# Spreading copies moved between row blocks, and one PSUM tile per bank for odd heads, in a softmax-times-V kernel

## The chip, the cores and the metric

One NeuronCore of a Trainium2 chip runs the kernel. The metric is device time in microseconds (us), as the median of several executions; times inside an execution come from its profile, counted from the start of the profiled span (about 2 us shorter than the device time). The engines are called PE (matmuls), PEld (the weight loads of PE), DVE (VectorE), ACT (ScalarE), POOL (GpSimd) and SP (which issues all DMAs here). The granted clock is the share of its full clock that PE was given, as the profile records it.

## The reference

```python
# scores: (8, 12, 1024, 1024) fp32, v: (8, 12, 1024, 64) fp32; 96 heads in all
attn = np.exp(scores - np.max(scores, axis=-1, keepdims=True))
attn = attn / (np.sum(attn, axis=-1, keepdims=True) + 1e-8)
return np.matmul(attn, v).astype(np.float32)
```

The kernel leaves out the maximum (the scores are normal draws) and gets the row sums from a column of ones beside v.

## The kernel before

The loop takes four heads per pass, 24 passes in all. A head has eight row blocks of 128 rows. For each block ACT makes exponentials in fp16 (`p_nat`, two blocks per instruction), PE transposes them in eight pieces into PSUM (`psT`), DVE copies them to SBUF (`pt`, "pt copy" below), and two blocks later PE multiplies them with v (`psO`). At the end of a head DVE normalises: one reciprocal and two multiplications into `out_sb`. The fourth head of a pass is normalised in two halves, after its fourth and its eighth block.

v arrives by one DMA per pass, on other partitions than the products need. Four small DVE copies per head ("spreading copies") move it there.

```python
psT_bufs = buffers(ps_pool, 4, [P, SK], FP16, "psT")            # 4 banks
psO_bufs = buffers(ps_pool, 2, [P, R // G, 512], FP32, "psO")   # 2 x 2 banks; R // G = 2
...
def normalise(k, st, first, last):
    psO = st["psO"][:, first:last, 0 : G * M].rearrange("p b (g m) -> p b g m", m=M)
    recip = st["recip"][:, first:last]
    nc.vector.reciprocal(out=recip, in_=psO[:, :, :, D : D + 1])
    ...                                     # T = 2 multiplications into out_sb
def finish(u):                              # products of one row block
    ...
    for c in range(C):
        nc.tensor.matmul(out=st["psO"][:, b, g * M : (g + 1) * M],
                         lhsT=pt[:, c * P : (c + 1) * P], rhs=st["vones"][:, c, 0:M], ...)
    if k == AHEAD - 1:                      # fourth head: bank by bank
        if g == G - 1:
            normalise(k, st, b, b + 1)
    elif r == R - 1:
        normalise(k, st, 0, R // G)
...
def spread_v(k):
    for s in range(S):                      # S = 4
        nc.vector.tensor_copy(
            out=vones_bufs[k][s * Q : (s + 1) * Q, :, 0:D].rearrange("i (h l) d -> i h l d", l=L),
            in_=v_half[k * Q : (k + 1) * Q, :, s])
def last(n0):                               # loads and store at the end of a pass
    ...                                     # last pass but one:
            load(AHEAD - 2, BH - 2, (4, 4))
            load(AHEAD - 1, BH - 1, (2, 2, 2, 1, 1))    # the last head's scores in five pieces
            store(n0, AHEAD - T)
def heads(n0):
    for k in range(AHEAD):                  # AHEAD = 4
        spread_v(k)
        st = dict(vones=vones_bufs[k])
        for r in range(R):                  # R = 8
            ...                             # exponentials, transposes into psT
            nc.vector.tensor_copy(out=pt[:], in_=psT[:])
            ...                             # finish() of the block two before
    ...
    cast_v()                                # POOL: v of the next pass to fp16
    last(n0)
```

Written once per head, the spreading copies depend on nothing that the pass makes, and the framework's scheduler puts all sixteen of a pass at its start.

The softmax here doesn't subtract the row's maximum and nothing guards it: scores larger than these inputs give would overflow.

## Time and profile before

| | before |
|---|---|
| device time, median | 1070.0 us (1069.4 to 1070.8) |
| DMA queue, share of 16 engines' span | 98.8% |
| DVE / ACT / PE / PEld busy | 73% / 69% / 67% / 62% |
| a spreading copy | 285 ns, 16 in a pass |
| a pt copy | 688 ns, 32 in a pass |
| last exponential ends | 1052.35 us |
| last multiplication ends | 1063.34 us |
| span | 1067.8 us |

The first two rows say that the run is a stream of bytes. The last three say that the work after the stream takes some 15 us, and only there can other engines show. The prediction shows the lines and reads them.

### The profile page before, as it was taken

The numbers are of one execution on the slowest core, as the hardware profiler recorded it, in microseconds if no ns is written. First come the engines' busy times: TensorE is split into PE (matmuls) and PEld (weight loads), VectorE is DVE, ScalarE is ACT, GpSimd is POOL, SyncE is SP. The second block draws the span as 40 slices with busy tenths as digits, with TensorE's granted clock in tenths as the row PEclk, the third lists the DMA queues.
The fourth block names the chain that finished last, engine by engine and source line by source line (L and its number), as shares of the span: only waits on it lengthen the run. The fifth ranks groups of instructions, "written<-read, shape, count | busy, mean of one in ns | idle before, by whom it ended". The sixth has DMA issues, their size and how long they took to land.

```text
span 1067.8 us, 32453 instructions
## 1 busy us (share of the span) xinstructions
PE 713.4 (67%) x12288; PEld 663.8 (62%) x12288; DVE 775.3 (73%) x1517; ACT 735.8 (69%) x432; POOL 48.1 (5%) x31
## 2 busy tenths in 40 slices
PE   3765757667676567665766757667676677675765
PEld 2755756656666567665766756656666566665665
DVE  3675867777677677777776867767777777777677
ACT  3756776666867667586666776666867667586684
POOL 0000000000000000000000000000000000000000
PEclk9888868898698897987878869888788787977889
DMA  9999999999999999999999999999999999999994
GB/s 393 431 425 434 422 442 432 432 432 429 435 431 432 432 432 425 439 432 432 432 431 434 424 440 432 432 432 430 434 432 432 432 432 426 438 432 432 432 425 173
DMA packets 24915, 453.05 MB, mean 424 GB/s; under 512 B 2768, under 2 KB 2768, under 8 KB 9168
## 3 DMA queue, kind: packets, MB, share of 16 engines
q1 hardware_dynamic: 24912, 453.00, 98.8%
q8 instruction: 3, 0.05, 0.0%
HBM read 436.21 MB, written 25.17 MB: 432 GB/s over the span
## 4 chain that ended last, share of the span: by engine, by line
DMA 78%; ACT 12%; PEld 4%; PE 2%; DVE 2%; issue 1%; SPq 0%; ACTq 0%; DVEq 0%; PEldq 0%
DMA s_nat<-in_scores_dram 78%; ACT p_nat L243 12%; PEld L255 3%; PEld L136 1%; PE psT L255 1%; DVE pt L261 1%; PE psO L136 1%; DVE vones L200 0%; SPq L176 0%; DVE out_sb L121 0%; ACTq L243 0%; SPq L188 0%; DVE recip L116 0%; DVEq L224 0%; PEldq L217 0%
## 5 line engine op out<-in xcount | busy, mean ns | idle before, releaser
L243 ACT ACTIVATE p_nat<-s_nat 128x2048 f16<-128x2048 f32 (+1 forms) x408 | 705.0, 1800 | 226.5 <-DMA s_nat<-in_scores_dram 200.6
L261 DVE COPY pt<-psT 128x1024 f16<-128x1024 f16 x768 | 511.3, 688 | 221.8 <-PE psO L136 96.7
L255 PE MATMUL psT<-order,p_nat 128*128 128x128 f16 x6144 | 550.2, 245 | 165.0 <-ACT p_nat L243 161.6
L255 PEld LDWEIGHTS <-p_nat 128*128 128x128 f16 x6144 | 441.2, 123 | 177.4 <-ACT p_nat L243 177.0
L136 PE MATMUL psO<-vones,pt 128*128 128x65 f16 x6144 | 356.7, 204 | 183.0 <-DVE pt L261 132.9
L136 PEld LDWEIGHTS <-pt 128*128 128x128 f16 x6144 | 291.5, 106 | 220.0 <-DVE pt L261 171.3
L121 DVE TENSOR_TENSOR out_sb<-psO,recip 64x512 f32<-64x512 f32 (+1 forms) x240 | 139.7, 582 | 7.8
L200 DVE COPY vones<-v_half 32x512 f16<-32x512 f16 x384 | 109.4, 285 | 23.2 <-POOL v_half L195 6.0
L243 ACT ACT_TABLE_LOAD x24 | 30.8, 1283 | 90.1 <-DMA s_nat<-in_scores_dram 82.0
L195 POOL CAST v_half<-v_sb 128x2048 f16<-128x2048 f32 x25 | 47.4, 1897 | 994.4 <-DMA v_sb<-in_v_dram 574.6
L116 DVE RECIPROCAL recip<-psO 128x8 f32<-128x8 f32 (+1 forms) x120 | 22.7, 189 | 34.0 <-PE psO L136 34.0
L71 DVE MEMSET vones<- 128x16 f16 x4 | 0.2, 72 | 0.8 <-PEq L295 0.8
L62 DVE CAST order<-ident 128x128 f16<-128x128 f32 x1 | 0.2, 227 | 0.4 <-POOL ident masks.py:199 0.4
masks.py:199 POOL TENSOR_SCALAR_AFFINE_SELECT ident<-ident 128x128 f32<-128x128 f32 x1 | 0.3, 294 | 0.1
masks.py:197 POOL MEMSET ident<- 128x128 f32 x1 | 0.2, 205 | 0.3 <-POOLq L295 0.3
L295 POOL MEMSET const-float32-0.0<- 128x1 f32 x1 | 0.1, 99 | 0.2 <-issue 0.2
L295 POOL MEMSET const-bfloat16-1.0<- 128x1 bf16 x1 | 0.1, 103 | 0.0
L295 POOL MEMSET const-uint8-127<- 128x1 uint8 x1 | 0.1, 103 | 0.0
L295 POOL MEMSET const-float32-1.0<- 128x1 f32 x1 | 0.1, 99 | 0.0
## 6 DMA issues: line engine op xcount, KB each, us to landing
s_nat<-in_scores_dram SPq DMA_DIRECT2D x96, 4096.0 KB, 36.0
v_sb<-in_v_dram SPq DMA_DIRECT2D x24, 1024.0 KB, 37.6
out_dram<-out_sb SPq DMA_DIRECT2D x48, 512.0 KB, 27.8
s_nat<-in_scores_dram SPq DMA_DIRECT2D x2, 2048.0 KB, 33.6
s_nat<-in_scores_dram SPq DMA_DIRECT2D x3, 1024.0 KB, 32.7
s_nat<-in_scores_dram SPq DMA_DIRECT2D x2, 512.0 KB
```

The source lines that it names most:

```text
L62: nc.vector.tensor_copy(out=order16[:].rearrange("p (t j) -> p t j", t=T), in_=ident32[:].rearrange("p (j t) -> p t j", t=T),)
L71: nc.vector.memset(vo[:, :, D : D + 2], 1.0)
L116: nc.vector.reciprocal(out=recip, in_=psO[:, :, :, D : D + 1])
L121: nc.vector.tensor_tensor(out=rows.rearrange("j (b g) d -> j b g d", g=G), in0=psO[part, :, :, 0:D], in1=recip[part].to_broadcast([W, last ...
L136: nc.tensor.matmul(out=st["psO"][:, b, g * M : (g + 1) * M], lhsT=pt[:, c * P : (c + 1) * P], rhs=st["vones"][:, c, 0:M], start=(c == 0), ...
L195: nc.gpsimd.tensor_copy(out=v_half[:], in_=v_sb[:])
L200: nc.vector.tensor_copy(out=vones_bufs[k][s * Q : (s + 1) * Q, :, 0:D].rearrange("i (h l) d -> i h l d", l=L), in_=v_half[k * Q : (k + 1) ...
L243: nc.scalar.activation(out=p_nat[:, g : g + rows, :].rearrange("p r (x v) -> p x r v", v=Q * L), in_=s_bufs[k][:, r + g : r + g + rows, :] ...
L255: nc.tensor.transpose(out=psT[:, c * P : (c + 1) * P], in_=p_row[:, c // L, c % L, :], identity=order16[:],)
L261: nc.vector.tensor_copy(out=pt[:], in_=psT[:])
L295: nc = _bacc.Bacc("TRN2", target_bir_lowering=False, num_devices=1)
```

## The change

Two things are intended: DVE should not hold up the first row blocks of a pass for 5 us of spreading copies, and PE should not wait for the normalising of one bank before it writes the other.

```diff
-    psO_bufs = buffers(ps_pool, 2, [P, R // G, 512], FP32, "psO")
+    psO_whole = ps_pool.tile([P, R // G, 512], FP32, name="psO_whole")
+    psO_banks = buffers(ps_pool, R // G, [P, 1, 512], FP32, "psO")
...
 def normalise(k, st, first, last):
-        psO = st["psO"][:, first:last, 0 : G * M].rearrange("p b (g m) -> p b g m", m=M)
+        psO = psO_whole if k % 2 == 0 else psO_banks[first]
+        psO = psO[:, :, 0 : G * M].rearrange("p b (g m) -> p b g m", m=M)
...
-        if k == AHEAD - 1:
+        if k % 2 == 1:
             if g == G - 1:
                 normalise(k, st, b, b + 1)
...
 def heads(n0):
         for k in range(AHEAD):
-            spread_v(k)
+            if k == 0:
+                for s in range(S):
+                    spread_v(k, s)
...
-                nc.vector.tensor_copy(out=pt[:], in_=psT[:])
+                copy = nc.vector.tensor_copy(out=pt[:], in_=psT[:])
+                if k < AHEAD - 1 and r % (R // S) == 0:
+                    spread_v(k + 1, r // (R // S), copy)
```

`spread_v(k, s, behind)` now makes one copy and, with `behind`, gives the scheduler an order edge (no semaphore): not before that pt copy. The PSUM use stays at eight banks. Not in the intent, but in the diff: the second head of a pass is now normalised in halves too.

## The prediction

> **What bounds the kernel now.** I read the page's slices and queue part first, because a kernel with four engines near 70% may be bound by none of them.
>
> ```profile
> DMA  9999999999999999999999999999999999999994
> GB/s 393 431 425 434 422 442 432 432 432 429 435 431 432 432 432 425 439 432 432 432 431 434 424 440 432 432 432 430 434 432 432 432 432 426 438 432 432 432 425 173
> q1 hardware_dynamic: 24912, 453.00, 98.8%
> ```
>
> The DMA engines are full in every slice but the last, at a flat 432 GB/s. The chain of work in order of time says the same for one pass of the loop (four heads):
>
> ```profile
> 922.24 1.92 ACT p_nat L243
> 925.88 3.78 ACT p_nat L243 x3
> 929.79 36.02 DMA s_nat<-in_scores_dram
> 965.92 1.92 ACT p_nat L243
> ```
>
> One pass is 965.92 - 922.24 = 43.68 us, of which a load of scores is 36 us. It moves 16.8 MB of scores, 1.05 MB of v and 1.05 MB of results: 18.9 MB / 432 GB/s = 43.7 us. So 24 x 43.68 = 1048 us are bytes, and nothing on VectorE can shorten them. What is left is the start (the first load is on its way at 2 us) and what follows the last byte. Next I cut the tail into windows (columns: stretch, length, busy time of PE, PEld, DVE, ACT, POOL, granted clock, DMA share, GB/s):
>
> ```profile
> 1046.00:1048.00 2.00, 2.00 (x45) 2.00 (x42) 1.93 (x4) 2.00 (x2) 0.00 (x0) 1.00 1.01 416
> 1048.00:1050.00 2.00, 1.08 (x23) 0.77 (x22) 1.97 (x4) 1.96 (x2) 0.00 (x0) 1.00 0.71 291
> 1054.00:1062.00 8.00, 4.89 (x106) 4.44 (x103) 6.64 (x13) 0.00 (x0) 0.00 (x0) 1.00 0.05 19
> 1064.00:1066.00 2.00, 0.00 (x0) 0.00 (x0) 0.00 (x0) 0.00 (x0) 0.00 (x0) 0.59 0.64 262
> ```
>
> The scores are in by about 1051, yet the span ends at 1067.8. DVE is the busiest engine in between (6.64 of 8 us). The timeline of the last pass (heads 92 to 95) shows why it is late:
>
> ```profile
> 1024.70 5.03 DVE L200 COPY vones<-v_half 32x512 f16<-32x512 f16 x16 [0.58 <-PE L255]
> 1029.76 1.89 DVE L261 COPY pt<-psT 128x1024 f16<-128x1024 f16 x3
> 1030.20 22.15 ACT L243 ACTIVATE p_nat<-s_nat 128x2048 f16<-128x2048 f32 x13 [1.09 <-DMA s_nat<-in_scores_dram]
> 1037.16 0.69 DVE L261 COPY pt<-psT 128x1024 f16<-128x1024 f16 x1 [0.27 <-PE L136]
> 1038.12 0.69 DVE L261 COPY pt<-psT 128x1024 f16<-128x1024 f16 x1 [0.27 <-PE L136]
> 1038.72 0.20 DVE L116 RECIPROCAL recip<-psO 128x8 f32<-128x8 f32 x1
> 1039.08 0.69 DVE L261 COPY pt<-psT 128x1024 f16<-128x1024 f16 x1 [0.15 <-PE L136]
> 1048.29 3.21 DVE L261 COPY pt<-psT 128x1024 f16<-128x1024 f16 x5
> 1060.16 1.18 PE L136 MATMUL psO<-vones,pt 128*128 128x65 f16 x32 [1.64 <-DVE out_sb L121]
> 1062.25 0.18 DVE L116 RECIPROCAL recip<-psO 128x4 f32<-128x4 f32 x1 [1.42 <-PE psO L136]
> ```
>
> Four things are to be seen. All sixteen spreading copies of the four heads run in one piece at the pass's start, not four per head, and hold the first pt copy until 1029.76. The exponentials of heads 93 to 95 run without a break and end at 1052.35, 8 us before the last pt copy (1060.14), so VectorE trails. A pt copy alone has 0.27 us idle before it (pitch 0.96), while in a run of several the pitch is 3.21/5 = 0.64; the reciprocal at 1038.72 fell into such a gap and the next copy still began 0.27 after the end of the one before (1038.12 + 0.69 + 0.27 = 1039.08), so small work fits in there. And the last head's products of row blocks 4 to 7 all wait, 32 of them, until bank 0 is normalised. This last wait is in every pass:
>
> ```profile
> PE psO L136 <- DVE out_sb L121: 43.7, 24, 2.0
> ```
>
> **What the Trainium skill says.** "DMA: Bandwidth & Descriptors", Specifications, has a fabric ceiling of 435 GB/s; the trace's 432 agrees, and is above the limit of about 358 GB/s for HBM per core in the same table, so here (one core running) the measurement decides. "PSUM — Partial Sum Buffer", PSUM bank collisions raise a hardware error, asks to guard by bank and quadrant and says that different banks run clean: so products into bank 1 need not wait for reads of bank 0, and the wait above comes of the tile spanning both. "VectorE: DVE Perf Modes", Side-by-side: where the cycles go, gives about 158 cycles at 0.96 GHz on top of the elements; as an estimate from that page, a spreading copy (512 fp16 at 4 per cycle) is (128 + 158)/0.96 = 298 ns and a pt copy out of PSUM (1024 at 2 per cycle) 698 ns; the groups have 285 and 688. It agrees, and says that a spreading copy is mostly fixed cost, so splitting them up gives no saving by itself. "TensorE: Matmul & The Clock Gate", What's actually happening, has half clock for some 3.4 us after idling: the trace has eight transposes' weight loads in 0.83 us at 1030.89 and in 0.48 us from 1034.26 on.
>
> **The change part by part.**
>
> Middle of the run: per pass it adds one reciprocal and two multiplications on VectorE (head 1 now in two halves): 2 x (0.178 + 2 x 0.423) - (0.197 + 2 x 0.688) = 0.48 us, and takes off PE's wait of 1.8 us. VectorE has 32.3 of 43.7 us busy in a pass, so both lie beside the loads: 0.
>
> Start: the first load is under way before any of it: 0.
>
> Tail, from 1024.70, along VectorE, which is the engine that trails:
> (a) Of sixteen spreading copies (pitch 5.06/16 = 0.316) four stay in front, so the first pt copy begins at 1024.70 + 1.26 = 1025.96. Three transposed blocks are there by then, as 1024.70 came after the first transposes. The exponentials of head 92 end at 1023.7, 25.5, 27.3, 29.1, a block per 0.9 us, and an isolated copy needs 0.96, with the spreading copies of head 93 in the gaps: eight copies x 0.97 end at 1033.7. Before, the eighth ended at 1037.16 - 0.27 = 1036.89: 3.2 us gained.
> (b) From there to the end of the last pt copy it was 1060.83 - 1036.89 = 23.94. Added: eight spreading copies, four I put in gaps (0.05 each) and four in closed-up runs (0.31 each), 1.45; the halves of head 93, 0.48. Taken off: after each normalising the next copies follow closely (seen at 1048.29), and there is one more normalising, so some three gaps of 0.3: -0.9. Sum +1.0.
> (c) From the last pt copy's end to the end of the last multiplication was 1063.34 - 1060.83 = 2.51, as 32 products take 2.06 us (1060.16 to 1062.22 in the chain). With only the last block's eight left: 8 x 0.064 = 0.51, some 0.3 of latency, the reciprocal and two multiplications 1.1: 1.9, so -0.6.
> (d) The last store, 1063.4 to 1067.8, stays.
> Sum: -3.2 + 1.0 - 0.6 = -2.8 us. I take 2.4 of it, because PE is at half clock for the first blocks of head 92 and may hold some copies of (a): 1070.0 - 2.4 = **1067.6**. A floor: the last exponential ends at 1052.35, and a block's transposes, copy, products and multiplications after it take some 3.7 us against the 11.0 of now (1063.34 - 1052.35), so more than 7.3 us cannot come of this.
>
> **The rivals.**
> R1, the gaps cannot be filled: a spreading copy moves to other partitions, and the pt copy behind it waits its 0.27 anew. Then each costs 0.316 or more wherever it stands, (a) is given back in (b), and only (c) stays: about 1069.5. For it: the spreading copies never overlap one another (0.316 pitch, 0.285 each). Against: the reciprocal at 1038.72 cost nothing.
> R2, PE's wait of 43.7 us in 24 passes is worth its length, and the time falls to about 1026. Against: DMA at 98.8%; bytes don't get fewer. I give it nothing.
> R3, a new wait before a load: the cast of v now has to wait for the last spreading copy, which moves from the start of the pass to the third head's end, and the next v load and the load behind it stand in order behind that cast. A DMA hole of 1 us per pass would be +24 us. Against: loads land 36 us after issue, more than three heads' worth stand in the queue, and v's own arrival already sets the cast in most passes (POOL waits for it 14 times of 24). I estimate the v load is issued 1 to 3 us later, which disappears in 36.
> R4, VectorE stops being the one that trails and exponentials bound the tail: the floor above, about 1063. It needs all gaps to close.
>
> **Range and chances.** R1 gives the upper end, 1069.7 with the run-to-run spread of 0.7 us; half-way to R4 the lower, 1065.6. Two per cent is 21 us: nothing in the tail is so long, and only R3 could do it the other way. Faster by over 2%: 0.01; within: 0.98; slower: 0.01.
>
> **What would show it.** Right: still 43.67 us from pass to pass and DMA all nines; spreading copies singly between pt copies, only four at 1024.7; first pt copy of the last pass near 1026; eighth ended near 1033.7; the wait of PE psO on out_sb gone from the list or down to a few us; eight products, not 32, before the last reciprocal; span about 1065.4. Wrong (a): the first pt copies of head 92 wait for PE. Wrong (b), R1: pitch from copy to copy over a spreading copy of 1.25 instead of 1.0. Wrong altogether: DMA below nine in a middle slice, or SP waiting for the cast longer than the queue is deep.

## The result, and the profile after

The changed kernel takes **1066.05 us** (median of 4, 1065.98 to 1066.48) against 1069.88 (median of 4) for the kernel before: 3.8 us less. The ratio is 0.9964, 95% interval 0.9947 to 0.9981. Ratios here are the mean time of one kernel's fast runs over that of the other's in the same rounds, so they are not quite the ratio of the medians. The time lies in the predicted range, 1.6 us under the predicted figure.

First the slices and the queue part of the changed kernel's page, and two lines of its chain of work in order of time:

```profile
DMA  9999999999999999999999999999999999999995
q1 hardware_dynamic: 24912, 453.00, 99.2%
```

```profile
929.60 36.07 DMA s_nat<-in_scores_dram
...
973.32 36.03 DMA s_nat<-in_scores_dram
```

The stream is as before: a pass takes 973.32 - 929.60 = 43.72 us. Next its timeline of the last pass (start, length, engine, line, what, count, and in brackets the idle time before and who ended it):

```profile
1024.12 1.23 DVE L208 COPY vones<-v_half 32x512 f16<-32x512 f16 x4 [0.58 <-PE L267]
1025.39 0.69 DVE L273 COPY pt<-psT 128x1024 f16<-128x1024 f16 x1
1026.11 0.28 DVE L208 COPY vones<-v_half 32x512 f16<-32x512 f16 x1
...
1031.76 0.69 DVE L273 COPY pt<-psT 128x1024 f16<-128x1024 f16 x1
...
1052.14 1.41 DVE L129 TENSOR_TENSOR out_sb<-psO_whole,recip 64x512 f32<-64x512 f32 x2 [0.74 <-DMA out_dram<-out_sb]
...
1057.07 0.69 DVE L273 COPY pt<-psT 128x1024 f16<-128x1024 f16 x1
1057.82 0.43 PE L145 MATMUL psO<-vones,pt 128*128 128x65 f16 x8 [1.21 <-DVE pt L273]
1058.48 0.18 DVE L124 RECIPROCAL recip<-psO 128x4 f32<-128x4 f32 x1 [0.72 <-PE psO L145]
```

Four spreading copies stand in front and not sixteen, the first pt copy begins at 1025.39 (before: 1029.76), and the eighth is the one at 1031.76. Eight products, not 32, come before the last reciprocal. One line is new: the multiplications of the third head wait 0.74 us for a store, the one of the pass before from the same buffer. Laid beside the prediction's points (us from the span's start):

| point in the last pass | before | predicted | after |
|---|---|---|---|
| spreading copies begin | 1024.70 | 1024.70 | 1024.12 |
| first pt copy begins | 1029.76 | 1025.96 | 1025.39 |
| eighth pt copy ends | 1036.89 | 1033.7 | 1032.46 |
| last pt copy ends | 1060.83 | 1058.6 | 1057.76 |
| last multiplication ends | 1063.34 | 1060.5 | 1059.57 |

The end moved by 3.77 us, which is the whole gain of 3.8.

### The profile page after: what moved, and what is told of

Its sections match the earlier page's. It is cut to its first block, busy times and chain, and to the rows that moved or that the text cites. A ratio compares the mean times of both kernels' runs of the same rounds, so it can differ in the third digit from the quotient of the medians.

```text
span 1064.1 us, 32213 instructions
## 1 busy us (share of the span) xinstructions
PE 734.8 (69%) x12288; PEld 682.6 (64%) x12288; DVE 786.6 (74%) x1589; ACT 735.8 (69%) x432; POOL 48.0 (5%) x31
## 4 chain that ended last, share of the span: by engine, by line
DMA 78%; ACT 13%; PEld 4%; PE 3%; DVE 1%; issue 1%; SPq 0%; ACTq 0%; DVEq 0%
DMA s_nat<-in_scores_dram 78%; ACT p_nat L255 13%; PEld L267 2%; PE psT L267 2%; PEld L145 1%; DVE pt L273 1%; PE psO_whole L145 1%; PE psO L145 1%; SPq L185 0%; DVE out_sb L129 0%; ACTq L255 0%; SPq L197 0%; DVE recip L124 0%; ACTq L227 0%; DVE vones L208 0%
## 5 line engine op out<-in xcount | busy, mean ns | idle before, releaser
L267 PE MATMUL psT<-order,p_nat 128*128 128x128 f16 x6144 | 578.0, 247 | 263.9 <-ACT p_nat L255 256.9
L267 PEld LDWEIGHTS <-p_nat 128*128 128x128 f16 x6144 | 449.9, 123 | 291.1 <-ACT p_nat L255 288.8
L145 PEld LDWEIGHTS <-pt 128*128 128x128 f16 x6144 | 303.1, 108 | 84.4 <-DVE pt L273 81.4
L145 PE MATMUL psO<-vones,pt 128*128 128x65 f16 x3072 | 177.9, 202 | 56.2 <-DVE pt L273 52.6
L145 PE MATMUL psO_whole<-vones,pt 128*128 128x65 f16 x3072 | 190.3, 212 | 3.3 <-DVE pt L273 2.9
L129 DVE TENSOR_TENSOR out_sb<-psO,recip 64x256 f32<-64x256 f32 x192 | 81.2, 423 | 6.1
L129 DVE TENSOR_TENSOR out_sb<-psO_whole,recip 64x512 f32<-64x512 f32 x96 | 66.1, 688 | 3.7 <-DMA out_dram<-out_sb 0.7
L124 DVE RECIPROCAL recip<-psO 128x4 f32<-128x4 f32 x96 | 17.1, 179 | 34.2 <-PE psO L145 17.8
L124 DVE RECIPROCAL recip<-psO_whole 128x8 f32<-128x8 f32 x48 | 9.7, 203 | 4.8 <-PE psT L267 4.0
```

The source lines that it names most:

```text
L129: nc.vector.tensor_tensor(out=rows.rearrange("j (b g) d -> j b g d", g=G), in0=psO[part, :, :, 0:D], in1=recip[part].to_broadcast([W, last ...
L145: nc.tensor.matmul(out=bank[:, g * M : (g + 1) * M], lhsT=pt[:, c * P : (c + 1) * P], rhs=st["vones"][:, c, 0:M], start=(c == 0), stop=(c ...
L267: nc.tensor.transpose(out=psT[:, c * P : (c + 1) * P], in_=p_row[:, c // L, c % L, :], identity=order16[:],)
```

## The experiments

Twelve kernels ran. Kernels share the runs of the kernel before; its median was 1069.9 to 1070.3. In the notes below "from the eighth to the 26th pt copy" is a stretch of the last pass, end to end, that lies before the wait for the store in every version; it takes 17.49 us in the kernel before, with 2.53 us of idle DVE in it, and 18.17 us in the changed one, with 1.00 us idle (summed from the timelines).

### 1. The two halves of the change, and the change again

The changed kernel once more, unchanged:

> The changed kernel once more, beside the two halves of the change on the same chip. My theory (T): all of its 3.8 us come after the last byte of the scores, in three terms read from the two traces: the eighth pt copy of the last pass ends 4.4 us earlier, 1.4 us of that are given back up to the last pt copy, and the end after that copy is 0.7 us shorter. Expected 1066.0, before 1069.9.

Measured: 1066.16 us (5 runs), before 1070.18 (9 runs), ratio 0.9964. It repeats.

Spreading copies one by one, products' tile as before:

```diff
 # the changed kernel with
+    psO_bufs = buffers(ps_pool, 2, [P, R // G, 512], FP32, "psO")   # and its uses as before
-        if k % 2 == 1:
+        if k == AHEAD - 1:
```

> Half of the change: the spreading copies one by one between row blocks, the products' tile over two banks as before. T: the first pt copies of the last pass come some 3.8 us earlier, 1.2 are given back, and the long end (32 products after the normalising, 2.5 us from the last pt copy to the last multiplication) stays: 1067.3. Rival R1 (a spreading copy costs the same wherever it stands, so all of the gain is the banks'): 1069.9, as before.

Measured: 1067.66 us, ratio 0.9975 (0.9961 to 0.9989), 2.5 us gained. The first pt copy begins at 1026.53; from the last pt copy's end to the last multiplication's it is still 2.53 us. The wait of PE for the normalising is still in this kernel's list of waits (total us, times, longest):

```profile
PE psO L142 <- DVE out_sb L127: 46.0, 24, 2.1
```

A tile per bank, spreading copies as before:

```diff
 # the changed kernel with
-            if k == 0:
-                for s in range(S):
-                    spread_v(k, s)
+            for s in range(S):
+                spread_v(k, s)
...
-                if k < AHEAD - 1 and r % (R // S) == 0:
-                    spread_v(k + 1, r // (R // S), copy)
```

> The other half: a tile per bank for odd heads (and head 1 normalised in two halves), all sixteen spreading copies in one piece at the pass's start. T: 0.6 us at the start of the last pass, as the pass before it ends earlier, 0.7 us at the end, less some 0.4 for the added halves: 1069.0. Rival R1: the whole gain, 1066.1. If the parts add up, the two gains sum to about 3.8.

Measured: 1069.24 us, ratio 0.9990 (0.9976 to 1.0003), 0.9 us by the medians, an interval that just reaches 1. That wait is gone from its list. The timeline of its DVE:

```profile
1024.37 5.03 DVE L208 COPY vones<-v_half 32x512 f16<-32x512 f16 x16 [0.58 <-PE L266]
1029.43 1.89 DVE L272 COPY pt<-psT 128x1024 f16<-128x1024 f16 x3
```

So the order of the copies is worth some 2.5 us of the 4.0 and the banks some 0.9; the sum is short by 0.6, not more than the spread between runs. The rival that gave all to the banks falls.

### 2. Does "one by one" matter?

```diff
-                if k < AHEAD - 1 and r % (R // S) == 0:
-                    spread_v(k + 1, r // (R // S), copy)
+                if k < AHEAD - 1 and r == R - 2:
+                    for s in range(S):
+                        spread_v(k + 1, s, copy)
```

> The changed kernel with the four spreading copies of a head in one piece behind the seventh pt copy of the head before, and not singly behind every other one. The work is the same; only the places differ. T (single copies disappear in idle time before pt copies, or while VectorE waits for exponentials): 0.5 to 1.0 us slower than the changed kernel, 1066.5 to 1067.0. Rival (only that they are not all in front matters): 1066.0.

Measured: 1066.20 us against 1066.16 for the changed kernel. My expectation was wrong. Its DVE timeline, in the third head of the last pass:

```profile
1045.15 2.48 DVE L273 COPY pt<-psT 128x1024 f16<-128x1024 f16 x4
1047.66 1.24 DVE L208 COPY vones<-v_half 32x512 f16<-32x512 f16 x4
1048.93 1.89 DVE L273 COPY pt<-psT 128x1024 f16<-128x1024 f16 x3
...
1052.24 1.41 DVE L129 TENSOR_TENSOR out_sb<-psO_whole,recip 64x512 f32<-64x512 f32 x2 [0.71 <-DMA out_dram<-out_sb]
```

From the eighth to the 26th pt copy it takes 17.27 us with 0.56 us idle, less than with single copies. That is no gain, though, for the first eight pt copies took 7.88 us here and 7.07 there. From the start of the first to the end of the 26th both take the same, 25.15 us here and 25.24 there. Then both meet the wait for the store (the multiplications begin at 1052.24 and 1052.14), which would have hidden a small difference from the device time. Single copies have no merit of their own that a run shows. What matters is that twelve of the sixteen no longer stand in front.

### 3. What do the spreading copies still cost?

All of them before the loop, none in it (the result is wrong):

```diff
-            if k == 0:
-                for s in range(S):
-                    spread_v(k, s)
...
-                if k < AHEAD - 1 and r % (R // S) == 0:
-                    spread_v(k + 1, r // (R // S), copy)
...
 # before the loop, after cast_v():
+    for k in range(AHEAD):
+        for s in range(S):
+            spread_v(k, s)
```

> The changed kernel with all spreading copies before the loop and none in it (wrong result on purpose): what they still cost where they stand now. T: in the last pass the first four in front and about six in closed-up runs of pt copies cost 0.3 each, the others nothing, and part of it is taken up by a wait for the store: 1.0 to 2.0 us faster than the changed kernel, 1064.0 to 1065.0. If all of them are free now: 1066.0. If each costs its full 0.31: 16 x 0.31 = 5, so 1061.

Measured: 1067.19 us, ratio 0.9974: 1.1 us **slower** than with the copies, by the medians. It was run at another time. None of the expectations held. Its DVE timeline:

```profile
1046.43 0.69 DVE L270 COPY pt<-psT 128x1024 f16<-128x1024 f16 x1 [0.27 <-PE psT L264]
1047.39 0.69 DVE L270 COPY pt<-psT 128x1024 f16<-128x1024 f16 x1 [0.27 <-PE L264]
...
1049.92 0.20 DVE L124 RECIPROCAL recip<-psO_whole 128x8 f32<-128x8 f32 x1
1052.32 1.41 DVE L129 TENSOR_TENSOR out_sb<-psO_whole,recip 64x512 f32<-64x512 f32 x2 [2.20 <-DMA out_dram<-out_sb]
1053.76 2.48 DVE L270 COPY pt<-psT 128x1024 f16<-128x1024 f16 x4
```

Two things are to be seen. The lone pt copies with 0.27 us before them are back: the stretch from the eighth to the 26th takes 17.75 us with 2.49 us idle, so the eight spreading copies in the changed kernel's 18.17 cost 0.42 us in all, where eight at 0.316 would be 2.5 (in experiment 2, with them in one piece, the stretch was shorter than without them). And the scheduler put the third head's normalising before the 27th pt copy (in the changed kernel it is behind it); in the trace that copy and those behind it begin only after the 2.20 us of waiting for the store. Fewer instructions ended later because of where one wait stood.

### 4. Is the lone copy's gap made by a wait of the program?

```diff
-    pt_bufs = buffers(sb_pool, 4, [P, SK], FP16, "pt")
+    pt_bufs = buffers(sb_pool, 8, [P, SK], FP16, "pt")
```

> The changed kernel with eight pt buffers in place of four. The program's pt copies that stand alone, with 0.27 us idle before them, are those that carry a wait on an earlier VectorE instruction (the pt copy four before, same buffer); those without it follow in 0.6 to 0.7 us. With eight buffers fewer of them carry it (5 in place of 13 of the 32 in a pass). Theory (that wait makes the gap): the gaps go where it goes, and the last pass ends 0.5 to 1.2 us earlier, about 1065.2. Rival (the gap is how long it takes to hear from PE, or ScalarE's pace): 1066.0, same gaps.

Measured: 1066.07 us, with the kernel before at 1069.86; no difference to the changed kernel, and none in the stretch before the wait for the store either: 18.26 us, 1.10 idle. The buffers did take waits away: in the traces 119 of all 768 pt copies carry a wait on DVE's own semaphore, in the changed kernel 270.

But the run could not test the theory, because the changed kernel hardly has the gap any more. Idle times of 0.25 to 0.29 us before a pt copy, counted in the traces: 200 in the kernel before, nine of them in its last pass, but 30 in the changed kernel and none in its last pass. For the theory: of those 200, 186 stand before a pt copy that carries a wait on DVE's own semaphore, which 358 of the 768 do; in experiment 3's kernel it is 184 of 211. Against it: of the changed kernel's 30 it is only 8, and several of its pt copies that carry such a wait follow at 0.6 us. Eight buffers in the kernel before would be the test, and were not run. What makes the 0.27 us stays open.

### 5. What is the change worth where DMA does not bound?

In both kernels the loads of scores inside the loop are left out; every pass uses the first four heads' scores (wrong). Loads of v and stores stay.

```diff
 def load_next(k, n0):
-        if k < AHEAD - 2:
-            load(...)
+        return
 # and in last(): no load(...), only load_v and store
```

> The kernel before with the loads of scores inside the loop left out (the first four heads' scores are used in every pass; the result is wrong on purpose), so that DMA no longer bounds it. T (in the kernel before, the change's gain is hidden behind the loads in 23 of 24 passes): a pass then takes what the engines need, some 38 us as in the last pass (1024.7 to 1063.3), so about 24 x 38 + 40 = 950. Rival: ScalarE, 30.6 us busy per pass, bounds both kernels and they come out alike near 800.

> The changed kernel with the same loads left out (wrong result on purpose). T: a pass takes some 34.7 us as in its last pass (1024.1 to 1059.6 less a wait for a store of 0.7), about 24 x 34.7 + 40 = 870, 8% under the kernel before without loads. Rival: no difference (ScalarE bounds both).

> Only the first half of the change (spreading copies one by one, products' tile over two banks as before), with the loads of scores in the loop left out (wrong result on purpose): which half is worth what once DMA does not bound. The kernels before and after measured 968.6 and 858.4 so. Theory (the spreading copies fill the idle time before lone pt copies, and the long block no longer holds PE and ScalarE): the larger part, some 70 of the 110 us, so 900; the wait of PE for the normalising, 39.4 us in 24 passes in the kernel before without loads, stays in its waits. Rival (the wait for the normalising is what counts): at most 30 us gained, 940 or more.

Measured: 968.6 us (kernel before), 858.4 (changed), 873.9 (spreading copies alone). The busy lines of the three pages, in this order:

```profile
PE 648.1 (67%) x12288; PEld 604.5 (63%) x12288; DVE 772.4 (80%) x1517; ACT 744.9 (77%) x432; POOL 48.0 (5%) x31
```

```profile
PE 647.3 (76%) x12288; PEld 575.0 (67%) x12288; DVE 766.3 (90%) x1589; ACT 744.0 (87%) x432; POOL 48.1 (6%) x31
```

```profile
PE 654.3 (75%) x12288; PEld 592.7 (68%) x12288; DVE 761.9 (87%) x1517; ACT 744.3 (85%) x432; POOL 48.1 (6%) x31
```

The same change is worth 110 us, 11%, once the bytes do not bound. DVE does nearly the same work in each; its idle time falls from 194.0 us (966.4 - 772.4) to 89.9 (856.2 - 766.3). The spreading copies' order makes 94.7 of the 110.2 us, more than I expected (some 70), and the tile per bank 15.5. PE's wait for the normalising, still 45.3 us in the third kernel's list of waits, was so worth a third of its length. The granted clock rose along with the gain (0.91, 0.97 and 0.94 in the three profiled runs, in this order); how much of the gain comes through it, these runs do not separate. The main question of a large change with a small effect is answered all the same: the gain is there in every pass, and in 23 of 24 it hides behind the loads.

### 6. The two waits left at the end

Normalising the first bank of an odd head after its last pt copy:

```diff
-            if g == G - 1:
-                normalise(k, st, b, b + 1)
+            if r == R - 3 or r == R - 1:
+                normalise(k, st, b if r == R - 1 else 0, b + 1 if r == R - 1 else 1)
```

> The changed kernel with bank 0 of an odd head normalised after the head's last pt copy and not before it. In the changed kernel the last pt copy (1057.07) stood behind the two multiplications of bank 0 (0.9 us), and VectorE then idled 0.7 us for the last products. Theory: the last pt copy comes 0.9 us earlier and the multiplications fill the idle time: 1065.2. Rival (the pt copy was waiting for PE anyway): 1066.0.

Measured: 1065.54 us, ratio 0.9957. The last pt copy ends at 1056.81 (changed kernel: 1057.76), the last multiplication at 1058.94 (1059.57). The copy's 0.9 us came, 0.6 reached the end.

The store of the pass before in front of the last two pieces of scores:

```diff
-                load(AHEAD - 1, BH - 1, (2, 2, 2, 1, 1))
+                load(AHEAD - 1, BH - 1, (2, 2, 2))
                 store(n0, AHEAD - T)
+                load(AHEAD - 1, BH - 1, (1, 1), 6)      # load() takes its first row block
```

> The changed kernel with the store of heads 90 and 91 queued before the last two pieces of the last head's scores and not behind them. In the changed kernel the normalising of head 94, which writes the same buffer, waited 0.74 us for that store (landed at 1052.1, behind all loads). Theory: the wait goes and the last multiplication ends up to 0.7 us earlier: 1065.4. Rival: the last scores land 1.2 us later, ScalarE waits for them, and nothing is gained, or up to 0.5 us lost.

Measured: 1065.86 us, ratio 0.9959. The wait for the store is gone from the list of waits, but the end came only 0.1 us earlier (1059.46). Its timelines of ACT and of DVE:

```profile
1051.10 1.06 ACT L255 ACTIVATE p_nat<-s_nat 128x1024 f16<-128x1024 f32 x1 [0.53 <-PE L267]
1052.32 1.06 ACT L255 ACTIVATE p_nat<-s_nat 128x1024 f16<-128x1024 f32 x1 [0.16 <-PE L145]
```

```profile
1024.62 1.23 DVE L207 COPY vones<-v_half 32x512 f16<-32x512 f16 x4 [0.67 <-PE L267]
...
1052.03 1.41 DVE L129 TENSOR_TENSOR out_sb<-psO_whole,recip 64x512 f32<-64x512 f32 x2
1053.47 1.88 DVE L273 COPY pt<-psT 128x1024 f16<-128x1024 f16 x3
```

The last two exponentials now wait, and the last begins at 1052.32, 1.15 us later than in the changed kernel (1051.17). The list names PE, but it is the scores: in the trace their last load, moved behind a store of 0.5 MB (1.2 us at 432 GB/s), lands at 1052.23. So the rival's "later scores" came, but DVE did not wait for them: it runs without a gap of 0.1 us from 1051.31 to the last pt copy's end. The theory's gain came too: from the 26th pt copy to the last it takes 6.42 us in place of 7.14. It does not show at the end because this execution's last pass began 0.5 us later (1024.62 against 1024.12). The edit did not make that, as far as the runs show: ACT's exponentials in the pass before (from 1009.73 against 1009.46) were late already, long before the store was issued (1023.98), and in the kernel with both edits, which has the same store order, the last pass begins at 1024.02. The five runs lie between 1065.24 and 1066.18.

Both together:

> Both of the former together: 0.9 + 0.7 us if they add up, 1064.4, a version that beats both kernels by a little. If one hides the other: 1065.2.

Measured: **1064.88 us**, ratio 0.9953 (0.9940 to 0.9967), correct, against 1066.16 for the changed kernel beside an equal kernel before (1070.18 in both). The end of its DVE timeline:

```profile
1051.57 1.41 DVE L129 TENSOR_TENSOR out_sb<-psO_whole,recip 64x512 f32<-64x512 f32 x2
1053.01 2.48 DVE L273 COPY pt<-psT 128x1024 f16<-128x1024 f16 x4
...
1057.59 0.88 DVE L129 TENSOR_TENSOR out_sb<-psO,recip 64x256 f32<-64x256 f32 x2
```

The last multiplication ends at 1058.47. The version beats the kernel before by 5.3 us and the changed one by 1.3 (none of its five runs is above 1065.49, none of the changed kernel's five below 1066.03); less than the 1.6 expected.

## Why the prediction was right

**What bounds.** Right: a pass stays at 43.7 us, and the end of DVE's work moved by as much as the time. Experiment 5 shows the counterpart, an 11% gain without the loads, so rival R2 (PE's wait worth its length) was rightly given nothing for this kernel.

**Term (a), reckoned -3.2, measured -4.43.** The mechanism was right, the size off by 1.2. About half, 0.58, is something I left out: the pass before also ends earlier, so DVE reaches its spreading copies at 1024.12 and not 1024.70. The banks do this alone to 0.33 (1024.37 in their kernel). The rest is the pace: I had all eight copies lone, at 0.97, and they took (1032.46 - 1025.39)/8 = 0.88, with the third following the second at 0.6 (1026.32 and 1026.92). The discount for PE's half clock was hardly needed: the fifth copy waited 0.18 us for PE (1028.81), and from then on PE was at its quick pace, eight weight loads in 0.48 us. One reading was wrong and did no harm: in the kernel before, the third block's transposes end at 1026.60, so not three but two blocks were there by 1025.96.

**Term (b), reckoned +1.0, measured +1.36.** That it came so near is partly luck, for three errors partly cancelled. Up to the 26th pt copy 0.68 was given back, where I had put 1.0. The eight spreading copies cost 0.42 us of it and not 1.45 (experiment 3), since idle time before pt copies went as they came. The halves of head 93 with the gaps that they should close, put at 0.48 - 0.9 = -0.42, came to +0.26 (17.75 us without spreading copies, 17.49 in the kernel before) or to nothing (17.49 with the banks alone). The other 0.68 arose behind the 26th copy, and is the wait for the store (0.74), which the prediction does not name. In the kernel before, DVE reached that multiplication at 1054.5, after the store's landing near 1052.1; once earlier, it meets it.

**Term (c), reckoned -0.6, measured -0.70.** Right, and with its mechanism: eight products and 0.72 us of waiting in place of 32 and 1.42.

**The sum**, -2.8, was cut to -2.4 for the half clock; measured -3.77. **R1** (gaps cannot be filled) is wrong: experiments 1 and 3. My picture behind (a) and (b), single copies each filling its own gap, is not shown, though: four in one piece did as well. **R3** (the cast) came true as a wait and harmless as a cost. SP's own list of waits after:

```profile
SPq L197 <- POOL v_half L204: 97.2, 23, 5.5
```

SP now waits 97.2 us in 23 passes for the cast, and the v load of one pass is issued at 966.48 and no longer at 962.46, 4 us later (I said 1 to 3). The load behind it waits for ACT anyway (973.32 against 973.48), and the queue never ran dry. **R4** did not come: the end is 7.4 us behind the last exponential (1059.57 - 1052.22), against the floor of 3.7.

## What to carry to other kernels

When DMA is full in every slice, read what follows the last byte separately: a reordering can be worth 11% without the loads and 0.4% with them, and only the tail tells what it does. Instructions that depend on little were put at the front of the loop body by this scheduler, where all sixteen held up the first pt copy; an order edge kept twelve of them back, and eight of those then cost 0.42 us. After each gain look for the next wait at the new time: a store queued behind all loads set a point at 1052 us that no speed-up of what comes before that wait could pass. And test a theory on a kernel that still shows the effect, which experiment 4 did not.

## What the Trainium skill lacked or had wrong

- "VectorE: DVE Perf Modes", The DRAIN you can't avoid: it says that the next op does not start until the pipe is empty, that one that is not held starts earlier, and that semaphores cost nothing extra. Here pt copies of 0.69 us follow one another at 0.61 (1053.57, 1054.18 and 1054.78 in the changed kernel) or, in strings, at 0.96 with 0.27 us idle, though by the timeline PE had made their inputs before (from 1035.24 on in the kernel before). The page has no word on the second state. In the kernel before, 186 of 200 such gaps stand before a pt copy that waits on DVE's own semaphore, so it may be that the semaphore is not free here; that is not shown, and the cause is open.
- "DMA: Bandwidth & Descriptors", Queues, rings and completion order: it says that descriptors are consumed in ring order, but not what this means for a store: one of 0.5 MB, issued at 1031.34 behind the last scores, was waited for until 1052.1, some 20.7 us, and a multiplication that writes the same buffer waited with it.
